# Up-projections by seven block products, and the gate through DRAM, in a two-layer encoder trunk

## The chip, the cores and the metric

The kernel runs on one core of a Trainium2 chip. The metric is the device time of one execution in microseconds (us). The kernel before ran twice, in 2821.73 and 2818.32 us; the median is 2820.03 us.

## The reference

The input x is [1024 positions, 1024 channels], float32, batch 1. There are two layers; layer 0 mixes positions by differential attention, layer 1 by windowed attention with grouped heads. After the mixer each layer has a gated MLP with a convolution over positions, then an embedding p of its own, projected and gated. In the reference's own words, with D = 1024 and D_FF = 2816:

```
def conv_ffn(h, w_up, conv_w, conv_b, w_down):
    u = h @ w_up
    up = jnp.pad(u, ((0, 0), (pad, pad), (0, 0)))
    u = sum(up[:, t:t + S] * conv_w[t] for t in range(CONV_WIDTH)) + conv_b
    gate, val = jnp.split(u, 2, axis=-1)
    return (jax.nn.silu(gate) * val) @ w_down
...
    h = h + mix
    h = h + conv_ffn(rms_norm(h, ffn_norm[i]), ...)
    gate = jax.nn.sigmoid(rms_norm(h, ple_norm[i]) @ ple_w_gate[i])
    h = h + (p[i] @ ple_w_proj[i]) * gate
return rms_norm(h, final_norm)
```

## The kernel before

Channels lie on the 128 partitions and positions along the free axis, so a row of tiles [128, 1024] holds 128 channels. Every float32 operand of a product is split into two float32r parts, hi (a cast, on ScalarE, L134) and lo (the difference, on VectorE or GpSimd, L140). `mm3` (L221) then makes three products for each pair: hi by hi, hi by lo, lo by hi (L229 to L231), each 128x128 by 128x512 into a PSUM bank.

The program goes through stages: the first norm with q, k and v of layer 0; the differential attention, 64 units of one head by 128 positions; the output projection `out_proj` (L937); the feed-forward stage `ffn` (L989); the layer's embedding with q, k, v of layer 1; the windowed attention; `out_proj` and `ffn` again; the last embedding and norm. `p_proj` (L1087) computes p @ ple_w_proj with 96 products and 16 transposes. It is a generator that is handed to both attentions as a side job: after each unit of attention one of its pieces is issued.

`out_proj` adds the projection to the residual, which comes back from DRAM (`spill`), and `norm_tile` splits h * g into hn (hi and lo, L448 and L449) and sums h * h; 1 / rms (`rstd`) is applied only later, to the products.

`ffn` has 22 column blocks j of 128. For each j, `up` loads the weight columns of the value and of the gate (1 MB), splits them, and makes for both column blocks and both halves of the positions 24 products. L1031 multiplies PSUM by rstd; the conv is one ScalarE pass (L1033) and two VectorE taps (L1037, L1041); silu is L1046, the gate's product L1047. The gated block is split into gh and gl, which stay in SBUF. After two j the products of the down-projection of the two blocks before follow (`down`), 16 sums of six products, which L1067 adds to the residual in SBUF. Up uses five PSUM banks and down three.

DMAs are issued by SyncE (SP) in program order. The order of the instructions on each engine is set when the program is built, by a scheduler that simulates time; a tile in a pool waits for the last reader of the buffer it takes.

## Time and profile before

| | |
|---|---|
| runs | 2821.73 and 2818.32 us, median 2820.03 |
| span of the profiled execution, first to last instruction | 2821.1 us |
| TensorE busy | 2742.1 us, 97% |
| VectorE, ScalarE, GpSimd busy | 1639.3, 1092.5, 901.0 us |
| feed-forward stage, first product of up to last residual add | 734.92 to 1488.58 and 1972.71 to 2724.09 us |
| granted TensorE clock, mean | 0.993 of full speed |

The page doesn't list the profiled execution's own time apart from its span; the span lies 0.6 us under the slower of the two runs. In a timeline each row is one or more instructions in sequence on one engine: start, duration, line, operation, output and inputs. In square brackets stands how long the engine had been idle and what it had waited for. A matmul's row lasts longer than the distance to the next, because products are pipelined: the distance of the starts counts. In a table of windows "(x290)" is the number of instructions.

### The profile page before, as it was taken

How to read it: one execution, taken by the hardware profiler on the slowest of the kernel's cores; microseconds unless marked ns; L12 is line 12 of the kernel's file. 1: busy time of each engine (PE TensorE's matmuls, PEld its weight loads, DVE VectorE, ACT ScalarE, POOL GpSimd, SP SyncE). 2: the span in 40 equal slices, each digit the busy share in tenths (PEclk: the TensorE clock that was granted, in tenths of full speed). 3: DMA queues.
4: the chain of work that ended last, by engine and by line, in shares of the span. 5: the costliest groups of instructions: out<-in, count | busy, mean ns of one | idle time of the engine just before them, and what ended most of it. 6: DMA issues, size and time to landing. Idle time of an engine off the chain costs nothing.

```text
span 2821.1 us, 32960 instructions
## 1 busy us (share of the span) xinstructions
PE 2742.1 (97%) x13134; PEld 2271.8 (81%) x13134; DVE 1639.3 (58%) x2010; ACT 1092.5 (39%) x1923; POOL 901.0 (32%) x555
## 2 busy tenths in 40 slices
PE   7999999999999999999999999999999999999998
PEld 6888888888888888888878788888888888888877
DVE  7540468885655555455477747774555555555574
ACT  5321576773422222222245527874322222222253
...
GB/s 222 165 164 135 156 126 108 87 23 71 60 45 46 46 59 46 45 45 45 45 45 131 140 185 186 83 72 72 60 45 48 57 45 45 45 45 46 45 72 100
DMA packets 182239, 233.30 MB, mean 83 GB/s; under 512 B 7092, under 2 KB 136261, under 8 KB 178373
## 3 DMA queue, kind: packets, MB, share of 16 engines
...
q10 hardware_dynamic: 624, 0.39, 0.0%
...
## 4 chain that ended last, share of the span: by engine, by line
PE 80%; DVE 13%; ACT 4%; issue 2%; POOL 1%; DMA 1%; SPq 0%; POOLq 0%; ACTq 0%; DVEq 0%
PE ps L229 23%; PE ps L230 23%; PE ps L231 23%; DVE c L1037 2%; PE ps L770 2%; DVE res L1067 2%; ACT e L738 1%; PE T L761 1%; PE T L902 1%; DVE sm L734 1%; PE S L732 1%; PE S L733 1%; DVE ss L674 1%; DVE c L1041 1%; DVE c L1047 1%
## 5 line engine op out<-in xcount | busy, mean ns | idle before, releaser
L140 POOL TENSOR_TENSOR wl<-wr,wh 128x1024 fp32r<-128x1024 f32 (+1 forms) x201 | 482.5, 2421 | 1479.7 <-ACT wh L134 1405.0
L229 PE MATMUL ps<-hn,wh 128*128 128x512 f32 x1952 | 761.3, 391 | 5.2 <-ACT wh L134 4.5
L230 PE MATMUL ps<-hn,wh 128*128 128x512 f32 x1952 | 760.8, 390 | 0.0
L231 PE MATMUL ps<-hn,wl 128*128 128x512 f32 x1952 | 741.4, 390 | 0.7 <-DVE wl L140 0.7
L229 PEld LDWEIGHTS ps<-hn,wh 128*128 128x128 f32 x1952 | 366.9, 188 | 84.8 <-ACT wh L134 6.7
L231 PEld LDWEIGHTS ps<-hn,wl 128*128 128x128 f32 x1952 | 366.5, 188 | 78.5 <-issue 1.4
L230 PEld LDWEIGHTS ps<-hn,wh 128*128 128x128 f32 x1952 | 366.8, 188 | 76.3 <-issue 0.5
L1031 DVE TENSOR_TENSOR us<-ps,rstd 128x512 f32<-128x512 f32 x176 | 121.6, 691 | 443.1 <-PE ps L231 441.6
L134 ACT CAST wh<-wr 128x1024 fp32r<-128x1024 f32 (+1 forms) x232 | 233.3, 1060 | 268.3 <-PE ps L230 253.5
L1067 DVE TENSOR_TENSOR res<-res,ps 128x512 f32<-128x512 f32 x352 | 234.8, 680 | 129.7 <-PE ps L231 129.7
L229 PE MATMUL ps<-gh,wh 128*128 128x512 f32 x704 | 279.0, 400 | 18.6 <-DVE res L1067 14.5
L1033 ACT ACTIVATE c<-us,conv 128x1024 f32<-128x1024 f32 x88 | 109.1, 1240 | 456.9 <-DVE us L1031 456.9
L230 PE MATMUL ps<-gl,wh 128*128 128x512 f32 x704 | 274.5, 390 | 0.0
L231 PE MATMUL ps<-gh,wl 128*128 128x512 f32 x704 | 274.5, 390 | 0.0
L1037 DVE SCALAR_TENSOR_TENSOR c<-us,conv,c 128x1023 f32<-128x1023 f32 x88 | 196.5, 2233 | 72.2 <-ACT c L1033 72.2
L734 DVE TENSOR_REDUCE sm<-S 128x1 f32<-128x1024 f32 x128 | 152.6, 1217 | 63.1 <-PE S L733 62.4
L229 PEld LDWEIGHTS ps<-gh,wh 128*128 128x128 f32 x704 | 132.0, 188 | 71.0 <-DVE res L1067 45.1
L738 ACT ACTIVATE e<-S,sm 128x1024 f32<-128x1024 f32 x128 | 142.5, 1116 | 78.1 <-DVE sm L734 75.1
L134 ACT CAST gh<-c 128x1024 fp32r<-128x1024 f32 x44 | 46.2, 1050 | 309.8 <-DVE c L1047 309.8
L231 PEld LDWEIGHTS ps<-gh,wl 128*128 128x128 f32 x704 | 132.1, 188 | 28.2
L750 POOL TENSOR_TENSOR e<-e,e 128x1024 f32<-128x1024 f32 x64 | 152.5, 2382 | 4.9
L230 PEld LDWEIGHTS ps<-gl,wh 128*128 128x128 f32 x704 | 132.2, 188 | 25.6 <-issue 0.2
...
## 6 DMA issues: line engine op xcount, KB each, us to landing
wr<-ffn_w_up SPq DMA_DIRECT2D x88, 512.0 KB, 4.4
...
qs<-rhl SPq DMA_DIRECT2D x32, 512.0 KB, 3.2
...
ks<-rhl SPq DMA_DIRECT2D x20, 512.0 KB, 3.1
spill<-res SPq DMA_DIRECT2D x16, 512.0 KB, 2.7
...
```

Of the source, the lines that this page charges most:

```text
L134: self.nc.scalar.copy(out, in_)
L140: eng.tensor_tensor(out, in_, f32(hi), op=ALU.subtract)
L229: self.nc.tensor.matmul(out, ah, bh, start=first, stop=False)
L230: self.nc.tensor.matmul(out, ah, bl, start=False, stop=False)
L231: self.nc.tensor.matmul(out, al, bh, start=False, stop=last)
L734: v.tensor_reduce(sm[:, a : a + 1], ps[:], axis=AX.X, op=ALU.max, negate=True)
L738: nc.scalar.activation(e[:], ps[:], AF.Exp, bias=sm[:, a : a + 1], accum_out=sm[:, 2 + a : 3 + a])
L750: nc.gpsimd.tensor_tensor(ea[:], ea[:], eb[:], op=ALU.add)
L1031: v.tensor_tensor(u[:, sl], ps[:], rstd[hf][:], op=ALU.mult)
L1033: nc.scalar.activation(c[:], u[:], AF.Identity, bias=self.convcol(layer, 3, f), scale=self.convcol(layer, 1, f),)
L1037: v.scalar_tensor_tensor(c[:, 1:], u[:, : S - 1], self.convcol(layer, 0, f), c[:, 1:], op0=ALU.mult, op1=ALU.add,)
L1067: v.tensor_tensor(self.res[dt][:, sl], self.res[dt][:, sl], acc[:], op=ALU.add)
```

## The change

The up-projection is seen as a product of 2x2 blocks: the weight [1024 input channels, value and gate] in two halves of the input channels by two column blocks, and the input in two halves of the channels by two halves of the positions. Seven block products of sums take the place of eight, of four matrix steps of three products each: 84 products for each j where there were 96.

`seven_inputs` makes normalised inputs first (L1004, with rstd), then the sums t1 to t4, and splits all of them. `seven_weights` makes for each j the weight sums (L1048, L1051, L1052, on GpSimd, for j < 2 on VectorE) and splits them (casts on ScalarE L1057, differences on VectorE L1058). `ffn_up` multiplies and combines the seven results from PSUM (L1143 to L1155, for j = 0 other lines); conv (L1162 to L1170), silu (L1175) and the gate's product (L1176) follow as before, and the gated block is written to DRAM (`gs`, L1177). `ffn_down` is a stage of its own: it reads the gated blocks (L1190), splits them, and in its first group takes the residual from DRAM (L1213). `p_proj` is no longer a side job; `projected` (L1378) runs it by itself between `out_proj` and the up stage. In `out_proj` hn is no longer made. Layer 1 is changed alike. Documentation strings are removed, so line numbers shift, and `dynamic_dma_scratch_size=1024` is set for the program.

```diff
--- before.py
+++ after.py
@@ -453,7 +451,8 @@
-        self.norm_split(st, kt, hf, src)
+        if st["slots"] is not None:
+            self.norm_split(st, kt, hf, src)
@@ -945,7 +944,7 @@
-        st = self.norm_begin(which, layer, hp, tp, [S_LOW, XO[0]])
+        st = self.norm_begin(which, layer, hp, tp, None)
@@ -985,51 +984,181 @@
+    def seven_inputs(self, layer, rstd, fp):
+        nc = self.nc
+        v = nc.vector
+        sub = ALU.subtract
+        out = {n: [] for n in ("b11", "b21", "b22", "t1", "t2", "t3", "t4")}
+        for kp in range(KT // 2):
+            n = []
+            for kt in (kp, kp + KT // 2):
+                t = fp.tile([P, 2, HS], F32, "t", self.nm("nh"))
+                g = self.gcol("ffn", layer, kt)
+                for hf in range(2):
+                    v.scalar_tensor_tensor(
+                        t[:, hf], self.res[kt][:, hf * HS : (hf + 1) * HS], g, rstd[hf][:],
+                        op0=ALU.mult, op1=ALU.mult,
+                    )
+                n.append(t)
+            n1, n2 = n
+            one = fp.tile([P, 2, HS], F32R, "q1", self.nm("q1"))
+            nc.scalar.copy(one[:, 0], n1[:, 0])
+            v.tensor_tensor(one[:, 1], n1[:, 0], f32(one[:, 0]), op=sub)
+            ta = fp.tile([P, 2, HS], F32, "t", self.nm("ta"))
+            tb = fp.tile([P, 2, HS], F32, "t", self.nm("tb"))
+            v.tensor_tensor(ta[:, 0], n1[:, 1], n1[:, 0], op=sub)
+            v.tensor_tensor(ta[:, 1], n2[:, 1], ta[:, 0], op=sub)
+            v.tensor_tensor(tb[:, 0], n1[:, 1], n2[:, 1], op=sub)
+            v.tensor_tensor(tb[:, 1], ta[:, 1], n2[:, 0], op=sub)
+            qa = self.resp.tile([P, 2, 2, HS], F32R, tag="res", name=self.nm("qa"))
+            qb = fp.tile([P, 2, 2, HS], F32R, "qb", self.nm("qb"))
+            qu = fp.tile([P, 2, 2, HS], F32R, "qu", self.nm("qu"))
+            for q, t in ((qa, ta), (qu, tb)):
+                nc.scalar.copy(q[:, 0], t[:])
+                v.tensor_tensor(q[:, 1], t[:], f32(q[:, 0]), op=sub)
+            nc.scalar.copy(qb[:, 0, 0], n2[:, 0])
+            nc.scalar.activation(qb[:, 0, 1], n2[:, 1], AF.Copy, scale=-1.0)
+            v.tensor_tensor(qb[:, 1, 0], n2[:, 0], f32(qb[:, 0, 0]), op=sub)
+            v.scalar_tensor_tensor(
+                qb[:, 1, 1], n2[:, 1], -1.0, f32(qb[:, 0, 1]), op0=ALU.mult, op1=sub
+            )
...
+    def seven_weights(self, raw, fp, hurry):
+        nc = self.nc
+        v = raw[:].rearrange("p (b c) -> p b c", b=4)
+        sf = fp.tile([P, 4, HS], F32, "sf", self.nm("sf"))
+        eng = nc.vector if hurry else nc.gpsimd
+        eng.tensor_tensor(
+            sf[:, 0:2], v[:, 2].unsqueeze(1).to_broadcast([P, 2, HS]), v[:, 0::3], op=ALU.add
+        )
+        eng.tensor_tensor(sf[:, 2], sf[:, 1], v[:, 0], op=ALU.add)
+        eng.tensor_tensor(sf[:, 3], sf[:, 2], v[:, 1], op=ALU.add)
+        out = {}
+        def split(src, names, tile_):
+            t = tile_[:].rearrange("p (e b c) -> p e b c", e=2, c=HS)
+            self.nc.scalar.copy(t[:, 0], src)
+            nc.vector.tensor_tensor(t[:, 1], src, f32(t[:, 0]), op=ALU.subtract)
+            for i, n in enumerate(names):
+                out[n] = (t[:, 0, i], t[:, 1, i])
+        big = lambda: self.ring.tile(
+            [P, WSZ], F32R, tag="wh" if self.flip() else "wl", name=self.nm("w7")
+        )
+        split(v[:, 0:2], ("a11", "a12"), big())
+        split(sf[:, 2:4], ("s2", "s4"), big())
+        split(sf[:, 0:2], ("s3", "s1"), big())
+        split(v[:, 3:4], ("a22",), fp.tile([P, 2 * HS], F32R, "wd", self.nm("wd")))
+        return out
+    def product(self, ps, w, x, kps, first, last):
...
+    def ffn_up(self, layer, x7, fp, psum, gs):
         nc = self.nc
...
+        kps = range(KT // 2)
+        for j in range(FT):
+            raw = self.ring.tile([P, WSZ], F32, tag="wr", name=self.nm("wr"))
+            r = raw[:].rearrange("p (t k c) -> p t k c", t=2, k=KT)
             for t in range(2):
+                nc.sync.dma_start(
+                    r[:, t],
+                    wu[:, (t * FT + j) * P : (t * FT + j + 1) * P].rearrange(
+                        "(k p) c -> p k c", p=P
+                    ),
+                )
+            w = self.seven_weights(raw, fp, j < 2)
+            bank = lambda: psum.tile([P, HS], F32, "ps", self.nm("ps"))
+            small = lambda: fp.tile([P, HS], F32, "e", self.nm("e"))
+            ug = fp.tile([P, S], F32, "t", self.nm("ug"))
+            uv = fp.tile([P, S], F32, "t", self.nm("uv"))
+            lo, hi = slice(0, HS), slice(HS, S)
+            pairs = {
+                "m1": ("a11", "b11"), "m2": ("a12", "b21"), "m3": ("s4", "b22"),
+                "m4": ("a22", "t4"), "m5": ("s1", "t1"), "m6": ("s2", "t2"), "m7": ("s3", "t3"),
+            }
+            def prod(ps, m, first=True):
+                a, b = pairs[m]
+                self.product(ps[:], w[a], x7[b], kps, first, True)
+            if j == 0:
...
+            else:
+                pa, pb, pc, pd, pe = (bank() for _ in range(5))
+                t1, t2, t3 = small(), small(), small()
+                prod(pa, "m1")
+                nc.scalar.copy(t1[:], pa[:])
+                prod(pb, "m6")
+                v.tensor_tensor(t2[:], pb[:], t1[:], op=ALU.subtract)
+                prod(pd, "m7")
+                v.tensor_tensor(t3[:], t2[:], pd[:], op=ALU.add)
+                prod(pc, "m5")
+                v.tensor_tensor(uv[:, hi], t3[:], pc[:], op=ALU.add)
+                prod(pa, "m2", False)
+                nc.scalar.copy(ug[:, lo], pa[:])
+                prod(pe, "m4")
+                v.tensor_tensor(uv[:, lo], t3[:], pe[:], op=ALU.subtract)
+                prod(pc, "m3", False)
+                v.scalar_tensor_tensor(
+                    ug[:, hi], t2[:], -1.0, pc[:], op0=ALU.mult, op1=ALU.subtract
+                )
+            cs = [None, None]
+            for t, u in ((1, uv), (0, ug)):
                 f = t * FT + j
...
+                c = fp.tile([P, S], F32, "t", self.nm("c"))
                 nc.scalar.activation(
@@ -1042,13 +1171,27 @@
-                cs.append(c)
+                cs[t] = c
...
+            nc.sync.dma_start(gs[j][:], cs[0][:])
+    def ffn_down(self, layer, gs, hp, tp, psum, which, nlayer, rc=None):
+        nc = self.nc
+        v = nc.vector
+        wd = self.io["ffn_w_down"][layer]
+        groups = FT // 2
+        st = self.norm_begin(which, nlayer, hp, tp, [S_LOW, XO[0]])
+        self.res = [None] * KT
+        gts = {}
+        def load(j):
+            raw = tp.tile([P, S], F32, tag="t", name=self.nm("gr"))
+            nc.sync.dma_start(raw[:], gs[j][:])
...
-            self.copy_hi(hi[:], cs[0][:])
-            self.sub_lo(v, lo[:], cs[0][:], hi[:])
+            self.copy_hi(hi[:], raw[:])
+            self.sub_lo(v, lo[:], raw[:], hi[:])
@@ -1056,7 +1199,7 @@
-                acc = psum.at(DOWN_BANKS[(hf * KT + dt) % 3], [P, HS], F32, self.nm("ps"))
+                acc = self.bank(psum)
@@ -1064,28 +1207,41 @@
-                v.tensor_tensor(self.res[dt][:, sl], self.res[dt][:, sl], acc[:], op=ALU.add)
+                if g == 0:
+                    self.rows_tile(self.res, dt, "res")
+                    old = tp.tile([P, HS], F32, tag="n", name=self.nm("old"))
+                    nc.sync.dma_start(old[:], self.spill[dt * P : (dt + 1) * P, sl])
+                    v.tensor_tensor(self.res[dt][:, sl], old[:], acc[:], op=ALU.add)
+                else:
+                    v.tensor_tensor(self.res[dt][:, sl], self.res[dt][:, sl], acc[:], op=ALU.add)
...
+        dblk = {}
+        def fetch(g):
+            self.hurry = g == 0
+            dblk[g] = self.wrows(wd, 2 * g * P, 2, 0, D)
+            self.hurry = False
+            for j in (2 * g, 2 * g + 1):
+                load(j)
+        fetch(0)
...
-            up(2 * g)
-            up(2 * g + 1)
-            if g > 0:
-                for hf in range(2):
-                    down(g - 1, hf, False)
-            dblk[g] = self.wrows(wd, 2 * g * P, 2, 0, D)
-        for hf in range(2):
-            down(groups - 1, hf, True)
-            self.norm_half(st, hf, psum, ["b4"])
-            if rc is not None:
-                self.rstd_cols(st["rstd"][hf], hf, rc, psum, ["b4"])
+            if g + 1 < groups:
+                fetch(g + 1)
+            for hf in range(2):
+                down(g, hf, g == groups - 1)
+                if g == groups - 1:
+                    self.norm_half(st, hf, psum, END_BANKS)
+                    if rc is not None:
+                        self.rstd_cols(st["rstd"][hf], hf, rc, psum, END_BANKS)
@@ -1214,10 +1370,34 @@
...
+    def projected(self, layer, w, out_pp, next_norm):
+        io = self.io
+        gs = [self.dram.tile([P, S], F32, name=self.nm("gs")) for _ in range(FT)]
+        with ExitStack() as c:
+            tp, hp = self.stage(c, f"w{layer}", XO[0] + XO[1])
+            psum = self.banks(c, f"w{layer}")
+            rstd = self.out_proj(w, hp, tp, psum, "ffn", layer)
+            self.spill_res()
+            for _ in self.p_proj(
+                layer, out_pp, psum, BANKS,
+                lambda n: tp.tile([P, S], F32, tag="t", name=n),
+            ):
+                pass
+        with ExitStack() as c:
+            fp = self.slots(
+                c, f"u{layer}",
+                {"q1": 4, "qb": 4, "qu": 4, "sf": 1, "wd": 2, "t": 5, "e": 4},
+            )
+            psum = self.slots(c, f"pu{layer}", {"ps": 8}, PSUM)
+            x7 = self.seven_inputs(layer, rstd, fp)
+            self.ffn_up(layer, x7, fp, psum, gs)
+        return gs
@@ -1271,19 +1451,13 @@
-            side = self.p_proj(
-                0, pp[0], psum, END_BANKS,
-                lambda n: ap.pools["e"].tile([P, S], F32, tag="e", bufs=EBUF, name=n),
-            )
-            self.diff_attn(ap, psum, [side])
+            self.diff_attn(ap, psum, [])
+        gs = self.projected(0, io["diff_w_o"][0], pp[0], "ple")
...
-                hn, rstd = self.ffn(0, hn, rstd, hp, tp, psum, "ple", 0)
+                hn, rstd = self.ffn_down(0, gs, hp, tp, psum, "ple", 0)
```

Three places show how instructions move. The first is VectorE where the up stage begins in layer 0; `wl`, `w_1121`, `w_1123`, `wd` are lo parts of weights, `nh` a normalised input, `sf` a weight sum, `nacc` the sum of squares. Before:

```order
L140 TENSOR_TENSOR wl_6462<-wr_6458,wh_6461 128x512 x2
L449 SCALAR_TENSOR_TENSOR hn_6345<-res_6167,par,hn_6345 128x512
L464 TENSOR_TENSOR nacc_5944<-nacc_5944,old_6342 128x512
L965 TENSOR_TENSOR res_6234<-ps_6383,old_6408 128x512
L464 TENSOR_TENSOR nacc_5944<-nacc_5944,old_6375 128x512
L140 TENSOR_TENSOR wl_6595<-wr_6591,wh_6594 128x512 x2
L449 SCALAR_TENSOR_TENSOR hn_6411<-res_6234,par,hn_6411 128x512
L464 TENSOR_TENSOR nacc_5944<-nacc_5944,old_6408 128x512
```

In the change, from the end of the norm's second half on:

```order
L468 SCALAR_TENSOR_TENSOR nv_6182<-nv_6182 128x512
L469 SCALAR_TENSOR_TENSOR rstd_6186<-nv_6182,rstd_6186 128x512
L1058 TENSOR_TENSOR w_1121_6527<-wr_6520,w_1121_6527 128x1024
L1004 SCALAR_TENSOR_TENSOR nh_6416<-res_5687,par,rstd_6056 128x512
L1004 SCALAR_TENSOR_TENSOR nh_6416<-res_5687,par,rstd_6186 128x512
L1004 SCALAR_TENSOR_TENSOR nh_6419<-res_5957,par,rstd_6056 128x512
L1004 SCALAR_TENSOR_TENSOR nh_6419<-res_5957,par,rstd_6186 128x512
L1048 TENSOR_TENSOR sf_6523<-wr_6520 128x1024
L1058 TENSOR_TENSOR wd_6536<-wr_6520,wd_6536 128x512
L1058 TENSOR_TENSOR wd_6671<-wr_6655,wd_6671 128x512
L1015 TENSOR_TENSOR ta_6425<-nh_6416 128x512
```

Ahead of the up stage VectorE now has no hn split left, and all work on the inputs follows after the second half's rstd, with weight work of j = 0 and 1 among it.

The second place is VectorE in the middle of the stage, one j. Before, with adds of the down-projection (`res`) between (`us` is the product times rstd, `c` the conv):

```order
L1031 TENSOR_TENSOR us_8374<-ps_8401,rstd_6420 128x512
L1067 TENSOR_TENSOR res_6018<-res_6018,ps_8590 128x512
L1067 TENSOR_TENSOR res_6167<-res_6167,ps_8606 128x512
L1037 SCALAR_TENSOR_TENSOR c_8427<-us_8374,conv,c_8427 128x1023
L1067 TENSOR_TENSOR res_6234<-res_6234,ps_8622 128x512
L1041 SCALAR_TENSOR_TENSOR c_8427<-us_8374,conv,c_8427 128x1023
L1047 TENSOR_TENSOR c_8370<-c_8370,c_8427 128x1024
L1067 TENSOR_TENSOR res_6234<-res_6234,ps_8614 128x512
L140 TENSOR_TENSOR gl_8434<-c_8370,gh_8433 128x1024
L1031 TENSOR_TENSOR us_8446<-ps_8447,rstd_6278 128x512
```

In the change (`e`, `ug` and `uv` are combinations of PSUM banks; `w_` and `wd` are lo parts of the weights of later j):

```order
L1147 TENSOR_TENSOR e_7076<-e_7075,ps_7072 128x512
L1153 TENSOR_TENSOR uv_7068<-e_7076,ps_7073 128x512
L1149 TENSOR_TENSOR uv_7068<-e_7076,ps_7071 128x512
L1058 TENSOR_TENSOR w_1232_7317<-wr_7310,w_1232_7317 128x1024
L1166 SCALAR_TENSOR_TENSOR c_7168<-uv_7068,conv,c_7168 128x1023
L1170 SCALAR_TENSOR_TENSOR c_7168<-uv_7068,conv,c_7168 128x1023
L1145 TENSOR_TENSOR e_7206<-ps_7201,e_7205 128x512
L1155 SCALAR_TENSOR_TENSOR ug_7067<-e_7075,ps_7071 128x512
L1058 TENSOR_TENSOR w_1216_7192<-sf_7182,w_1216_7192 128x1024
L1166 SCALAR_TENSOR_TENSOR c_7172<-ug_7067,conv,c_7172 128x1023
L1170 SCALAR_TENSOR_TENSOR c_7172<-ug_7067,conv,c_7172 128x1023
L1176 TENSOR_TENSOR c_7172<-c_7172,c_7168 128x1024
```

The adds of the down-projection and the split of the gate have left, and a j now has four weight differences and five combinations.

The third place is the queue of DMAs on SP between up and down of layer 0. Before, in the same stage, weight loads alternate:

```order
L161 DMA wr_7126<-ffn_w_up 128x8x128 x2
L161 DMA wr_7255<-ffn_w_up 128x8x128 x2
L161 DMA wr_7512<-ffn_w_down 128x2x1024
L161 DMA wr_7520<-ffn_w_up 128x8x128 x2
L161 DMA wr_7649<-ffn_w_up 128x8x128 x2
L161 DMA wr_7906<-ffn_w_down 128x2x1024
```

In the change, from the last but one gated block on (`gs` the gated blocks in DRAM, `gr` their read, `old` the residual from `spill`):

```order
L1177 DMA gs_5523<-c_9268 128x1024
L159 DMA wr_9863<-ffn_w_down 128x2x1024
L1177 DMA gs_5524<-c_9399 128x1024
L1190 DMA gr_9519<-gs_5503 128x1024
L1190 DMA gr_9525<-gs_5504 128x1024
L1190 DMA gr_9539<-gs_5505 128x1024
L1190 DMA gr_9545<-gs_5506 128x1024
L1213 DMA old_9559<-spill_6192 128x512
L1213 DMA old_9569<-spill_6192 128x512
L1190 DMA gr_9723<-gs_5507 128x1024
...
L1213 DMA old_9580<-spill_6192 128x512
```

The first reads of gated blocks stand behind the write of the last one, and most loads of the residual behind the reads of four more.

## Rows read from the trace of the kernel before

**Rows 1.** Page, part 1: busy time, share of span, instructions of each engine.
```profile
PE 2742.1 (97%) x13134; PEld 2271.8 (81%) x13134; DVE 1639.3 (58%) x2010; ACT 1092.5 (39%) x1923; POOL 901.0 (32%) x555
```

**Rows 2.** Windows, feed-forward stage: us, then each engine's busy time, PEclk, DMA, GB/s.
```profile
1008.68:1075.75 67.07, 66.18 (x290) 53.82 (x289) 34.73 (x36) 15.01 (x15) 14.29 (x7) 1.00 0.16 47
```

**Rows 3.** Timeline of PE in up: start us, us, operation; 18 products left out.
```profile
1001.64 0.39 PE L231 MATMUL ps<-hn,wl 128*128 128x512 f32 x1
...
1005.95 0.39 PE L231 MATMUL ps<-hn,wl 128*128 128x512 f32 x1
```

**Rows 4.** Timeline of POOL, the same stage: a weight block's subtraction.
```profile
1008.68 4.76 POOL L140 TENSOR_TENSOR wl<-wr,wh 128x1024 fp32r<-128x1024 f32 x2 [22.48 <-ACT wh L134]
```

**Rows 5.** Timeline of DVE, the same stage.
```profile
1009.09 0.69 DVE L1067 TENSOR_TENSOR res<-res,ps 128x512 f32<-128x512 f32 x1 [0.67 <-PE ps L231]
1011.06 3.46 DVE L1037 SCALAR_TENSOR_TENSOR c<-us,conv,c 128x1023 f32<-128x1023 f32 x1
...
1015.04 1.27 DVE L1041 SCALAR_TENSOR_TENSOR c<-us,conv,c 128x1023 f32<-128x1023 f32 x1
```

**Rows 6.** Timeline of PE: first product of up, layer 0 and layer 1.
```profile
734.92 0.39 PE L229 MATMUL ps<-hn,wh 128*128 128x512 f32 x1
...
1972.71 0.39 PE L229 MATMUL ps<-hn,wh 128*128 128x512 f32 x1
```

**Rows 7.** Timeline of DVE: last residual add of down, layer 0 and 1.
```profile
1488.58 0.68 DVE L1067 TENSOR_TENSOR res<-res,ps 128x512 f32<-128x512 f32 x1
...
2724.09 0.68 DVE L1067 TENSOR_TENSOR res<-res,ps 128x512 f32<-128x512 f32 x1
```

**Rows 8.** Timeline of POOL in layer 0's attention, one L750 for each unit.
```profile
375.91 2.37 POOL L750 TENSOR_TENSOR e<-e,e 128x1024 f32<-128x1024 f32 x1
...
400.29 2.37 POOL L750 TENSOR_TENSOR e<-e,e 128x1024 f32<-128x1024 f32 x1
...
435.80 2.36 POOL L750 TENSOR_TENSOR e<-e,e 128x1024 f32<-128x1024 f32 x1
...
456.06 2.36 POOL L750 TENSOR_TENSOR e<-e,e 128x1024 f32<-128x1024 f32 x1
```

**Rows 9.** Windows: layer 1's attention.
```profile
1760.00:1860.00 100.00, 98.64 (x606) 87.41 (x605) 82.24 (x146) 89.04 (x246) 44.94 (x80) 1.00 0.19 67
```

**Rows 10.** Groups of one shape: count, busy, mean ns; then idle before, releaser.
```profile
L1033 ACT ACTIVATE c<-us,conv 128x1024 f32<-128x1024 f32 x88 | 109.1, 1240 | 456.9 <-DVE us L1031 456.9
...
L140 DVE TENSOR_TENSOR gl<-c,gh 128x1024 fp32r<-128x1024 f32 x44 | 53.6, 1218 | 14.8 <-ACT gh L134 14.8
...
L134 ACT CAST gh<-c 128x1024 fp32r<-128x1024 f32 x44 | 46.2, 1050 | 309.8 <-DVE c L1047 309.8
```

**Rows 11.** DMA view, issues: count, KB each, us from issue to landing.
```profile
pp<-pp SPq DMA_DIRECT2D x16, 512.0 KB, 2.6
old<-spill SPq DMA_DIRECT2D x32, 256.0 KB, 2.7
```

**Rows 12.** Timeline of DVE: back to back ops, and a wait for ScalarE.
```profile
741.52 0.74 DVE L449 SCALAR_TENSOR_TENSOR hn<-res,par,hn 128x512 fp32r<-128x512 f32 x1
742.18 0.68 DVE L464 TENSOR_TENSOR nacc<-nacc,old 128x512 f32<-128x512 f32 x1
...
749.00 0.68 DVE L1031 TENSOR_TENSOR us<-ps,rstd 128x512 f32<-128x512 f32 x1
749.60 0.68 DVE L469 SCALAR_TENSOR_TENSOR nv<-nv 128x512 f32<-128x512 f32 x1
...
1335.20 1.28 DVE L1037 SCALAR_TENSOR_TENSOR c<-us,conv,c 128x1023 f32<-128x1023 f32 x1 [1.37 <-ACT c L1033]
```

**Rows 13.** Windows after a pause of PE in layer 1's attention.
```profile
1875.00:1880.00 5.00, 5.00 (x22) 4.14 (x21) 2.94 (x7) 2.93 (x6) 1.87 (x3) 0.69 0.00 0
```

**Rows 14.** Timeline of PE in that window.
```profile
1876.79 0.78 PE L229 MATMUL ps<-wh,wh 128*128 128x512 f32 x1
1877.36 0.63 PE L230 MATMUL ps<-wl,wh 128*128 128x512 f32 x1
```

More of the change, by code (lines that the diff above doesn't have):

```diff
@@ L102 @@
 MIX_BANKS = ["b4", "b2", "b5", "b3"]
-UP_BANKS = ["b0", "b1", "b6", "b7", "b4"]
-DOWN_BANKS = ["b5", "b2", "b3"]
 class Trunk:
@@ L986, in half_order @@
             done(hf)
-    def ffn(self, layer, hn, rstd, hp, tp, psum, which, nlayer, rc=None):
+    def seven_inputs(self, layer, rstd, fp):
[36 more added lines that the diff above has]
+            )
+            out["b11"].append((one[:, 0], one[:, 1]))
+            for name, q, i in (
+                ("b21", qb, 0), ("b22", qb, 1), ("t1", qa, 0),
+                ("t2", qa, 1), ("t3", qu, 0), ("t4", qu, 1),
+            ):
+                out[name].append((q[:, 0, i], q[:, 1, i]))
+        return out
@@ new lines, in flip @@
+    def flip(self):
+        self.turn = not getattr(self, "turn", False)
+        return self.turn
+    def product(self, ps, w, x, kps, first, last):
+        terms = [
+            (w[0][:, k * P : (k + 1) * P], w[1][:, k * P : (k + 1) * P], x[k][0], x[k][1])
+            for k in kps
+        ]
+        n = len(terms)
+        for i, (ah, al, bh, bl) in enumerate(terms):
+            mm = self.nc.tensor.matmul
+            mm(ps, ah, bh, start=first and i == 0, stop=False, skip_group_check=True)
+            mm(ps, ah, bl, start=False, stop=False, skip_group_check=True)
+            mm(ps, al, bh, start=False, stop=last and i == n - 1, skip_group_check=True)
@@ L1281, in run @@
             with ExitStack() as c:
-                psum = self.banks(c, "w0")
-                hn, rstd = self.out_proj(io["diff_w_o"][0], hp, tp, psum, "ffn", 0)
-            with ExitStack() as c:
                 psum = self.banks(c, "f0")
-                hn, rstd = self.ffn(0, hn, rstd, hp, tp, psum, "ple", 0)
+                hn, rstd = self.ffn_down(0, gs, hp, tp, psum, "ple", 0)
             with ExitStack() as c:
@@ L1294, in run @@
             psum = Bank(c, self.tc, "ps_a1", ["S0", "b2", "b3", "b4", "b5", "S1"], PSUM)
-            side = self.p_proj(
-                1, pp[1], psum, MIX_BANKS,
-                lambda n: ap.pools["a"].tile([P, S], F32, tag="a", bufs=6, name=n),
-            )
-            self.swa(ap, psum, [side])
+            self.swa(ap, psum, [])
+        gs = self.projected(1, io["swa_w_o"][0], pp[1], "ple")
         with ExitStack() as sc:
@@ L1302, in run @@
             with ExitStack() as c:
[L1303 to L1305 removed]
                 psum = self.banks(c, "f1")
                 rcol = self.cp.tile([P, 8], F32, name="rcol2")
[L1308 removed]
+                hn, rstd = self.ffn_down(1, gs, hp, tp, psum, "ple", 1, rcol)
             with ExitStack() as c:
```

69 lines of the change are left out of this document (25 added, 44 removed).

## The prediction, made before the changed kernel ran

> **What bounds the kernel now.** First the page's busy row [rows 1]: TensorE is busy 97% of the 2821.1 us span, so a change is worth what it takes off TensorE less the pauses it makes. Then the table of windows in the feed-forward stage [rows 2]: one group (two column blocks j of the up-projection and one group of the down-projection, 288 products) lasts 67.07 us. A product of 512 columns starts every (1005.95 - 1001.64) / 19 = 0.2268 us [rows 3]; 288 of them are 65.3 us, so only 1.8 us in 67 (2.7%) is lost. Where it is lost the timelines of VectorE and GpSimd show: from 1008.68 GpSimd subtracts for 4.76 us [rows 4], and the conv tap L1037 that starts at 1011.06 takes 3.46 us where the next takes 1.27 [rows 5]; the adds L1067 that free the down-projection's banks queue behind it. The add at 1009.09, which reads PSUM, takes 0.69 us though GpSimd is busy. So an instruction of VectorE with both operands in SBUF waits for GpSimd's, and one on PSUM does not.
>
> The stage runs from its first product to its last residual add: 734.92 to 1488.58 and 1972.71 to 2724.09 [rows 6, 7], that is 753.7 and 751.4 us, 1505.0 together. There is no pause ahead of it: the first up-product follows out_proj's last at once.
>
> **What is removed.** Per block j 84 products stand for 96: 12 x 22 x 2 = 528 fewer, 528 x 0.2268 = 119.7 us. The multiplications by 1/rms (L1031) go, and so do the stalls at three down banks, as the down stage has eight. The side job p_proj leaves both attentions. Layer 0: with it four units (the L750 at 375.91 to that at 400.29) take 24.4 us, later without it 20.3 (435.80 to 456.06) [rows 8], 1.03 us for each of 16 to 20 units: 18 us, between 16 and 20.6. Layer 1 has it nearly throughout; there TensorE is busy 98.6 of 100 us and ScalarE 89 [rows 9]. Its 96 products and the transposes are 22.8 us, the upper end; if ScalarE's chain sets the pace it gives nothing, the lower. I take 12. Together -30.
>
> **What is added, per layer.**
> *p_proj by itself*: 96 x 0.2268 = 21.8, some 1 for 16 transposes and 2 for its first casts (estimates): 24.8.
>
> *First pause, p_proj to up.* VectorE's first normalising op (L1004) writes to a tile of the next pool, in the memory that p_proj's output tiles held, so it waits for the last output transfer: about 1.05 us for the ScalarE cast ahead [rows 10], 0.6 for the PSUM copy (half of the 1.24 of a 1024-wide pass [rows 10]), 2.6 for the transfer [rows 11] and hops, 4.6 us after p_proj's last product. Everything of seven_inputs and of the first weights is queued behind it on VectorE: 20 ops like L449 at 0.66 (741.52 to 742.18), 30 of 512 columns at 0.60 (749.00 to 749.60) [rows 12], 13 subtractions of 1024 at 1.22 [rows 10]: 13.2 + 18.0 + 15.9 = 47.1, and 2 for ScalarE's casts between. Of the 168 products of j = 0 and 1 about 108 (24.5 us) can run meanwhile, as their operands come. TensorE stands 4.6 + 47.1 + 2 - 24.5, and 2 for the last operand's chain: 31. Low clock comes on top: after its pause before 1876 us TensorE had a granted clock of 0.69 (partly the 1.2 GHz level), and products started 0.57 us apart (1876.79, 1877.36) for some us [rows 13, 14]; that costs about 2.5 us. **34** in all, between 28 and 44.
>
> *Up.* j = 0 and 1: 168 x 0.2268 = 38.1. The other 20 cost 84 x 0.2268 = 19.05 each if TensorE sets the pace. VectorE's list for one j is three subtractions and the gate product at 1.22, one of 512 at 0.69, four conv taps at 1.28, five combinations from PSUM at 0.69: 4.9 + 0.7 + 5.1 + 3.5 = 14.2. GpSimd's three weight sums are 2 x 2.38 = 4.76 by [rows 4], and where they meet SBUF work one side waits: 18.96 at most, just under 19.05. I take the loss that the stage has now, 2.7%: 19.56 x 20 = **391.2**. The bounds are 19.05 and the rival below.
>
> Here a page speaks against the change. The Trainium skill (GPSIMD Engine Reference, 4.1 Engine selection) says to do an elementwise sum on VectorE, as GpSimd takes about twice as long for two inputs, and (8. Key points) that the two share SBUF interfaces when a VectorE op has two SBUF inputs. The trace agrees on both: 2.38 against 1.22 us, and 3.46 against 1.27. By that rule, with the sums on VectorE, the list would be 14.2 + 2.4 = 16.6 us, clear of 19.05.
>
> *Second pause, up to down.* After the last product of j = 21 come the last combination (0.69), conv on ScalarE (1.24) behind casts (1.05 each), two taps (1.28 each) that take turns with GpSimd's 2 x 2.38, silu (taken as a cast, 1.05), gate product (1.22): about 10.5 us by [rows 4, 5, 10]. On SP the reads of the first gate blocks are queued behind the write of this last one, so they are issued only now: 2.7 us to land [rows 11], a cast and hops: TensorE restarts after about 15. The residual's loads stand behind four block reads and have two buffers: (2.7 + 0.7) / 2 = 1.7 us each against 6 x 0.2268 = 1.36 of a down sum, 0.34 x 14 = 4.8 lost, less if the eight banks absorb it. With 2.5 of clock: **22**, between 14 and 32.
>
> *Down.* 1056 x 0.2268 = 239.5. Its end is VectorE's: norm work beside the adds as now, about 9.
>
> The DRAM trip of the gate costs nothing inside a stage: one 512 KB write takes 2.6 us [rows 11] and has a period of 19.6 us to itself, and a read is issued a group ahead; uncovered it would cost that 2.6, as it does in the second pause. VectorE and ScalarE lose the split of hn in out_proj, where TensorE is never idle: nothing.
>
> **Sum.** 24.8 + 34 + 38.1 + 391.2 + 22 + 239.5 + 9 = 758.6 per layer, 1517.2 for two against 1505.0: +12.2, less 30 in attention: -17.8. The profiled span becomes 2803.3. The span lies 1.1 us above the median of 2820.03 (runs of 2818.32 and 2821.73), so the median becomes **2802 us**: the 120 us that the products save are spent at two new pauses and on p_proj by itself.
>
> **Rivals.**
> 1. *The saving goes through* (13%). The up period is 19.05 (-10.2 a layer), the pauses 28 and 14 (-14), and attention gives 43.4 (-13.4): 2802 - 48.4 - 13.4 = 2740. For it: TensorE loses only 2.7% now. Against it: every term at its good end at once.
> 2. *VectorE becomes the bound in up* (20%), slower than before. Its list and GpSimd's sum to 18.96, and twice for each j VectorE waits for ScalarE's conv: at 1335.20 it had stood 1.37 us for that [rows 12]. If nothing fills these waits the period is 18.96 + 2.74 = 21.7, and 40 x (21.7 - 19.56) = 86 more: 2888. It decides from 21.4 a block, where the time passes 2% above now. By the two rules of the Trainium skill above (GPSIMD Engine Reference) the sums on GpSimd are the wrong side to put them. The trace bears out the sharing, not that the waits stay empty. Against it: the order puts other subtractions of the next block between.
> 3. *Longer pauses* (15%): 44 and 32, that is +20 a layer: 2842. For it: both sit behind transfers and one VectorE queue with no other work to run. It stays within 2%.
> My own case has 52%.
>
> **Numbers.** A measurement of this kernel tells about 2% (56 us) from no change, so faster is below 2764 and slower above 2876. Faster 0.13 (rival 1), slower 0.20 (rival 2), within 0.67 (forecast and rival 3). The range 2750 to 2890 takes in rival 3, rival 2 at its price and most of rival 1. The forecast's own range is 2775 to 2840.
>
> **What would show it.** Attention units of 5.07 us from the first one in layer 0; TensorE idle for about 31 us after p_proj's last product, with the first L1004 released by a transfer; 84 products every 19.1 to 20 us in up, without a wait for L1058 or for a bank longer than 0.5 us; TensorE idle for some 15 to 20 us before the down stage, released by the gate block's read; then 21.8 us for each down group. The prediction is wrong if the up period is above 21 us (VectorE releases TensorE at every block), or if either pause is outside its bounds.

## The result

The changed kernel takes 2790.16 us (2789.81 and 2790.52), the kernel before 2820.03. The ratio is 0.989, interval 0.9862 to 0.9919: 30 us less, within the 2% that count as no change here. The forecast was 2802, in a range from 2750 to 2890.

The page of the changed kernel, span and part 1, answers to [rows 1]:

```profile
span 2788.7 us, 33239 instructions
...
PE 2644.0 (95%) x12606; PEld 2183.4 (78%) x12606; DVE 1958.8 (70%) x2314; ACT 1210.2 (43%) x2101; POOL 1016.0 (36%) x587
```

TensorE's busy time fell by 98 us, the span by 32.4. VectorE is busy 320 us longer, its waits for GpSimd counted. Where the rest went is read at the stage's borders, as in [rows 6, 7]. The timeline of TensorE in layer 0 has the first work of p_proj, its last product, the first of up, the last of up and the first of down:

```profile
722.59 0.60 PE L1256 MATMUL ps<-identr,wr 128*128 128x128 f32 x4
...
748.83 0.39 PE L229 MATMUL ps<-wh,wl 128*128 128x512 f32 x1
754.89 0.80 PE L1084 MATMUL ps<-q,w 128*128 128x512 f32 x1 [5.67 <-ACT q L1011]
...
1201.25 0.39 PE L1086 MATMUL ps<-qb,w 128*128 128x512 f32 x1
1217.86 0.79 PE L227 MATMUL ps<-gh,wh 128*128 128x512 f32 x1 [16.22 <-ACT gh L132]
```

The same five in layer 1:

```profile
1935.46 0.71 PE L1256 MATMUL ps<-identr,wr 128*128 128x128 f32 x5
...
1962.34 0.39 PE L229 MATMUL ps<-wh,wl 128*128 128x512 f32 x1
1968.35 0.80 PE L1084 MATMUL ps<-q,w 128*128 128x512 f32 x1 [5.62 <-ACT q L1011]
...
2414.66 0.39 PE L1086 MATMUL ps<-qb,w 128*128 128x512 f32 x1
2431.15 0.80 PE L227 MATMUL ps<-gh,wh 128*128 128x512 f32 x1 [16.10 <-ACT gh L132]
```

The last residual adds on VectorE in both layers:

```profile
1476.08 0.69 DVE L1216 TENSOR_TENSOR res<-res,ps 128x512 f32<-128x512 f32 x1 [0.51 <-PE ps L229]
...
2692.14 0.69 DVE L1216 TENSOR_TENSOR res<-res,ps 128x512 f32<-128x512 f32 x1 [3.02 <-PE ps L229]
```

A last product occupies 0.23 us more than its start. With that the terms of the prediction come out as follows (us):

| term | predicted | layer 0 | layer 1 |
|---|---|---|---|
| p_proj by itself | 24.8 | 26.5 | 27.1 |
| pause ahead of up and thin first blocks | 34 | 33.3 | 33.2 |
| 22 blocks of up | 429.3 | 419.1 | 419.1 |
| second pause, down and its end | 270.5 | 274.6 | 277.3 |
| sum | 758.6 | 753.5 | 756.7 |
| sum before | | 753.7 | 751.4 |

The second row is the time from p_proj's end to up's end, less 22 x 19.05, so whatever up loses stands in it; where that lies follows below. The two stages together are 5.1 us longer than before (12.2 forecast). All the gain lies ahead of the two stages, where the attentions are: out_proj's last product is reached 12.3 us sooner in layer 0 and a further 24.8 in layer 1, together 37.1 (30 forecast). 37.1 - 5.1 and 0.4 behind the last add make the 32.4.

**Up** runs at TensorE's pace. One block in the window view, to be held against [rows 2]:

```profile
930.01:949.05 19.04, 19.04 (x86) 15.77 (x85) 16.67 (x15) 7.96 (x10) 7.82 (x3) 1.00 0.28 83
```

84 products of up are 19.04 us, and TensorE is busy in all of it, as in the whole 318.84 us from 861.16 to 1180.00. VectorE is busy 16.67 us, with its waits for GpSimd in it. In the timeline of VectorE a free conv tap, then one beside GpSimd, and the gate product (answers to [rows 5]):

```profile
936.85 1.28 DVE L1170 SCALAR_TENSOR_TENSOR c<-uv,conv,c 128x1023 f32<-128x1023 f32 x1
...
942.12 3.30 DVE L1170 SCALAR_TENSOR_TENSOR c<-ug,conv,c 128x1023 f32<-128x1023 f32 x1
946.62 1.22 DVE L1176 TENSOR_TENSOR c<-c,c 128x1024 f32<-128x1024 f32 x1 [1.19 <-ACT c L1175]
```

GpSimd's three weight sums in the same stretch:

```profile
941.01 3.33 POOL L1048 TENSOR_TENSOR sf<-wr 128x1024 f32<-128x1024 f32 x1 [11.07 <-DVE w L1058]
944.42 2.16 POOL L1051 TENSOR_TENSOR sf<-sf,wr 128x512 f32<-128x512 f32 x1
946.66 2.33 POOL L1052 TENSOR_TENSOR sf<-sf,wr 128x512 f32<-128x512 f32 x1
```

The tap at 942.12 takes 3.30 us, the one at 936.85 takes 1.28; the first sum takes 3.33. Both engines wait in turn, and at this length of the lists TensorE does not notice: it is busy in all of the 19.04 us.

**The pause ahead of up**, windows of layer 0 (columns as in [rows 2]):

```profile
722.00:740.00 18.00, 16.81 (x79) 13.03 (x78) 7.36 (x10) 12.54 (x20) 5.18 (x2) 1.00 0.63 196
740.00:760.00 20.00, 11.04 (x44) 8.13 (x43) 7.79 (x11) 9.37 (x15) 0.00 (x0) 0.86 0.41 165
760.00:780.00 20.00, 15.59 (x39) 9.65 (x39) 20.00 (x28) 8.27 (x11) 0.00 (x0) 0.63 0.19 52
780.00:800.00 20.00, 16.56 (x56) 10.97 (x56) 20.00 (x29) 8.72 (x11) 0.00 (x0) 0.91 0.19 52
```

TensorE is busy 11.04, 15.59 and 16.56 of 20 us, partly at 1.2 GHz (clock 0.86, 0.63, 0.91), while VectorE, from 753 on, works without a gap. On ScalarE the first weight cast, and on VectorE the first and the last operations of its queue:

```profile
749.07 1.04 ACT L1057 CAST w<-wr 128x1024 fp32r<-128x1024 f32 x1 [0.55 <-PE ps L228]
750.15 1.22 DVE L1058 TENSOR_TENSOR w<-wr,w 128x1024 fp32r<-128x1024 f32 x1 [15.13 <-ACT w L1057]
753.43 2.74 DVE L1004 SCALAR_TENSOR_TENSOR nh<-res,par,rstd 128x512 f32<-128x512 f32 x4 [2.06 <-DMA pp<-pp]
...
799.93 1.23 DVE L1024 TENSOR_TENSOR qu<-tb,qu 128x1024 fp32r<-128x1024 f32 x1
```

VectorE had stood 15.13 us, for a weight cast that waits for a ring tile until p_proj's last products have read it, and 2.06 more for the transfer of p_proj's last output. rstd had been ready at 735.0. The queue on the inputs ends at 801.16; by then TensorE has made 101 products of up in 52.1 us, so 29.2 of the 33.3 us are lost here. Another 2.1 go in a later block that waits for its weights (1.32 us at 838.04), and 1.8 in the last block, which waits for VectorE (1.65 us at 1198.58).

**The second pause** on SP, VectorE and ScalarE:

```profile
1208.45 0.37 SPq L159 DMA_DIRECT2D wr<-ffn_w_down  x1
1211.94 0.34 SPq L1177 DMA_DIRECT2D gs<-c  x1
1212.37 2.91 SPq L1190 DMA_DIRECT2D gr<-gs  x4
```

```profile
1206.26 3.24 DVE L1170 SCALAR_TENSOR_TENSOR c<-ug,conv,c 128x1023 f32<-128x1023 f32 x1
1210.69 1.23 DVE L1176 TENSOR_TENSOR c<-c,c 128x1024 f32<-128x1024 f32 x1 [1.18 <-ACT c L1175]
```

```profile
1216.76 1.04 ACT L132 CAST gh<-gr 128x1024 fp32r<-128x1024 f32 x1 [6.10 <-DMA gr<-gs]
```

The last gate product runs at 1210.69, its write is issued at 1211.94, the four reads behind it from 1212.37, and the first cast follows at 1216.76, after its transfer. TensorE stands 16.22 us.

### The profile page after: what moved, and what is told of

It is laid out like the page before. It is cut to its first block, busy times and chain, and to the rows that moved or that the text cites. A ratio compares the mean times of both kernels' runs of the same rounds, so it can differ in the third digit from the quotient of the medians.

```text
span 2788.7 us, 33239 instructions
## 1 busy us (share of the span) xinstructions
PE 2644.0 (95%) x12606; PEld 2183.4 (78%) x12606; DVE 1958.8 (70%) x2314; ACT 1210.2 (43%) x2101; POOL 1016.0 (36%) x587
## 5 line engine op out<-in xcount | busy, mean ns | idle before, releaser
L138 POOL TENSOR_TENSOR wl<-wr,wh 128x1024 fp32r<-128x1024 f32 (+1 forms) x113 | 293.1, 2609 | 817.6 <-ACT wh L132 743.9
L1048 POOL TENSOR_TENSOR sf<-wr 128x1024 f32<-128x1024 f32 x40 | 128.4, 3210 | 585.3 <-DVE w L1058 585.3
L1216 DVE TENSOR_TENSOR res<-res,ps 128x512 f32<-128x512 f32 x320 | 216.6, 684 | 140.4 <-PE ps L229 140.4
L227 PE MATMUL ps<-hn,wh 128*128 128x512 f32 x544 | 214.7, 396 | 5.6 <-ACT wh L132 4.9
L228 PE MATMUL ps<-hn,wh 128*128 128x512 f32 x544 | 212.9, 392 | 0.0
L229 PE MATMUL ps<-hn,wl 128*128 128x512 f32 x544 | 212.4, 392 | 0.1
L132 ACT CAST wh<-wr 128x1024 fp32r<-128x1024 f32 (+1 forms) x140 | 144.9, 1091 | 121.5 <-PE ps L228 62.7
L132 ACT CAST gh<-gr 128x1024 fp32r<-128x1024 f32 x44 | 46.2, 1050 | 343.3 <-PE ps L229 328.9
L1057 ACT CAST w<-sf 128x1024 fp32r<-128x1024 f32 x88 | 92.6, 1052 | 174.4 <-PE ps L1086 106.6
L229 PEld LDWEIGHTS ps<-gh,wl 128*128 128x128 f32 x704 | 133.0, 189 | 27.9
L749 POOL TENSOR_TENSOR e<-e,e 128x1024 f32<-128x1024 f32 x64 | 152.3, 2380 | 5.2
L1084 PE MATMUL ps<-qa,w 128*128 128x512 f32 x352 | 138.6, 397 | 10.5 <-ACT qa L1023 8.1
L1084 PE MATMUL ps<-qb,w 128*128 128x512 f32 x352 | 140.2, 398 | 6.0 <-DVE uv L1149 3.3
L1086 PE MATMUL ps<-qa,w 128*128 128x512 f32 x352 | 138.9, 395 | 2.6 <-DVE w L1058 2.6
L1085 PE MATMUL ps<-qa,w 128*128 128x512 f32 x352 | 139.3, 396 | 0.0
```

The lines of the kernel that those rows point to most:

```text
L132: self.nc.scalar.copy(out, in_)
L138: eng.tensor_tensor(out, in_, f32(hi), op=ALU.subtract)
L227: self.nc.tensor.matmul(out, ah, bh, start=first, stop=False)
L228: self.nc.tensor.matmul(out, ah, bl, start=False, stop=False)
L229: self.nc.tensor.matmul(out, al, bh, start=False, stop=last)
L749: nc.gpsimd.tensor_tensor(ea[:], ea[:], eb[:], op=ALU.add)
```

## The experiments

Each ran beside the kernel before, and the ratio to it is what is compared; the changed kernel has 0.989. The diffs are shortened: `...` stands for lines and arguments left out.

**1. p_proj back into the attentions.**

```diff
-            for _ in self.p_proj(...): pass
...
-            self.diff_attn(ap, psum, [])
+            self.diff_attn(ap, psum, [side])
...
-            self.swa(ap, psum, [])
+            self.swa(ap, psum, [side])
```

> p_proj goes back into both attentions as a side job; all else as changed. Theory (the terms of the prediction with their measured sizes): the two stages of p_proj by itself (26.5 us each, 722.59 to 749.06) go, -53; the attentions give back what they gained, +12.3 and +24.8; and the norm chain of about 12 us after out_proj's last product (rstd ready at 735.0) is no longer covered by TensorE work, which makes the pause ahead of up about 8 us longer in each layer, +16. Sum 0: 2790, between 2782 and 2798. Rival: what p_proj costs by itself is pure loss and its work was nearly free in attention: 2750 to 2765.

Measured: 2793.15 us, ratio 0.9894 (0.9879 to 0.9909). The attentions reach out_proj's end 16.9 and 27.9 us later, and the stages are 19.3 and 20.7 shorter. They are not 26.5 shorter, as TensorE now stands while the norm is made:

```profile
739.22 0.39 PE L229 MATMUL ps<-xo,wl 128*128 128x512 f32 x1
741.83 1.67 PE L488 MATMUL ps<-nacc,ones 128*128 128x512 f32 x2 [2.22 <-DVE nacc L463]
750.50 0.80 PE L1084 MATMUL ps<-q,w 128*128 128x512 f32 x1 [7.00 <-ACT q L1011]
```

From 739.22 to 750.50 there are only two products of the norm. So p_proj in the attentions costs 44.8 us and by itself, with what it covers, 40.0; taking it out moved the time and saved nothing that can be told apart. The theory holds; the prediction's size of layer 1's share does not (12 was forecast).

**2. The wait for p_proj's transfer taken away.** Another tile order in the pool:

```diff
+        qus = [fp.tile([P, 2, 2, HS], F32R, "qu", self.nm("qu")) for _ in range(KT // 2)]
...
-            qu = fp.tile([P, 2, 2, HS], F32R, "qu", self.nm("qu"))
+            qu = qus[kp]
```

> The tiles t3, t4 of the inputs take the memory in which p_proj's output tiles lay, so the normalised inputs no longer wait for p_proj's last output transfer; order of work unchanged. Theory: the wait alone is worth what VectorE stood for it, 2.06 us in each layer: 2786, since VectorE's queue behind it and the weight split ahead of it stay. Rival: the transfer sets the whole 6 us in which TensorE stands before its first up product, and the queue behind it moves by as much: 2778 or less.

Measured: 2787.04, ratio 0.9872 (0.9855 to 0.9888), whose interval overlaps the changed kernel's. VectorE's timeline:

```profile
749.98 1.23 DVE L1059 TENSOR_TENSOR w<-wr,w 128x1024 fp32r<-128x1024 f32 x1 [15.15 <-ACT w L1058]
751.12 1.41 DVE L1005 SCALAR_TENSOR_TENSOR nh<-res,par,rstd 128x512 f32<-128x512 f32 x2
```

No wait stands ahead of the normalisation any more, and the first up product comes 30.4 us after out_proj's last and not 32.5: the 2.1 us of the theory, at the start of up. They do not last. Up's last product comes 478.3 and 477.4 us after out_proj's last where it came 478.9 and 479.4, as the third and fourth gate product of layer 0 come 1.6 us later than this start would have them, and the whole stages are only 0.0 and 0.8 us shorter in the profiled execution. So it is shown that the wait delayed the start of up, not that it cost 2.1 us a layer; the times alone don't tell it either.

**3. p_proj beside the work on the inputs.**

```diff
-            for _ in self.p_proj(...): pass
...
             x7 = self.seven_inputs(layer, rstd, fp)
+            for _ in self.p_proj(layer, out_pp, psum, BANKS, fp):
+                pass
```

p_proj's results also leave in halves of 512 columns.

> p_proj is issued after the work on the inputs, in the same pool (its results leave in halves of 512 columns), so VectorE normalises and sums from the moment rstd is there, about 735 us, and not from 753, while TensorE does p_proj. Theory: VectorE's queue of 47 us is what fills the pause, so 18 us of it move under p_proj, of which some is lost as p_proj's own four VectorE subtractions come later: -15 to -18 in each layer, 2754 to 2760. Rival: the weights of the first block (ring tiles that p_proj holds to its end) or ScalarE's casts set the start of up: 2782 or more.

Measured: 2766.46, ratio 0.9799 (0.9784 to 0.9813): 24 us less than the changed kernel, and between the theory and the rival. The windows of the same stretch:

```profile
722.00:740.00 18.00, 12.57 (x46) 9.02 (x45) 12.73 (x14) 10.67 (x15) 5.46 (x2) 0.81 0.42 124
740.00:760.00 20.00, 17.86 (x77) 14.19 (x76) 20.00 (x31) 16.00 (x26) 0.00 (x0) 0.98 0.63 227
760.00:780.00 20.00, 19.47 (x75) 14.38 (x75) 20.00 (x26) 8.07 (x12) 0.00 (x0) 0.94 0.35 98
780.00:800.00 20.00, 18.85 (x80) 14.47 (x80) 18.51 (x22) 9.89 (x11) 6.18 (x3) 1.00 0.14 39
```

VectorE is full from 740 to 780, and TensorE is busy 17.86, 19.47 and 18.85 of 20. p_proj's first product, its last, and up's first:

```profile
730.92 0.50 PE L230 MATMUL ps<-wh,wh 128*128 128x512 f32 x1 [1.89 <-ACT wh L135]
...
755.84 0.39 PE L232 MATMUL ps<-wh,wl 128*128 128x512 f32 x1
757.19 0.50 PE L1087 MATMUL ps<-q,w 128*128 128x512 f32 x1 [0.96 <-ACT w L1060]
```

From out_proj's last product to the last add it is 742.5 and 745.0 us, against 753.7 and 756.9 in the changed kernel: 11 to 12 us a layer, under the 15 to 18 expected. p_proj itself ends later, at 756.1 and not at 749.1, mostly because it starts later: its first product comes 9.0 us after out_proj's last and not 2.5, since the norm's two products now stand ahead of its transposes and the norm's two activations ahead of its weight casts on ScalarE. VectorE's queue on the inputs starts at 734.69 and ends at 786.21, where it ran from 753.43 to 801.16, and the pause shrinks with it. That this queue sets the pause is shown by its place in time; no run made the queue itself shorter.

**4. The reads of gated blocks issued early**, on top of experiment 2.

```diff
-            nc.sync.dma_start(gs[j][:], cs[0][:])
+            (nc.scalar if j >= FT - 2 else nc.sync).dma_start(gs[j][:], cs[0][:])
...
-            self.nc.sync.dma_start(view, src)
+            (self.nc.scalar if self.late else self.nc.sync).dma_start(view, src)
```

(`late` is set for the third and fourth down weights.)

> As the run without the wait, and in addition the last two gate writes and the loads of the third and fourth down weights are issued by ScalarE, so that SP issues the first reads of gated blocks and of the residual without standing behind them. Theory: TensorE's second pause of 16.4 us shrinks by what the reads come earlier, to the last gate product plus one cast: about 12 us, and the next three blocks are there already: -5 to -7 in each layer against the run without the wait, 2772 to 2776. Rival: the pause is the chain conv, silu, gate product, cast on VectorE and ScalarE, and the transfer is a small part of it: within 2 us a layer, 2782 or more.

Measured: 2780.48, ratio 0.9851 (0.9837 to 0.9866): 6.6 us under experiment 2, which ran on the same chip. That is about half of the theory's 5 to 7 in each layer, and above its 2772 to 2776. SP issues the reads 8.6 us ahead of up's last product and not 11.1 behind it, and the pause is 11.8 us:

```profile
1189.58 3.33 SPq L1192 DMA_DIRECT2D gr<-gs  x4
```

```profile
1198.16 0.39 PE L1088 MATMUL ps<-qb,w 128*128 128x512 f32 x1
1210.32 1.22 PE L228 MATMUL ps<-gh,wh 128*128 128x512 f32 x2 [11.77 <-ACT gh L133]
```

```profile
1209.22 3.88 ACT L133 CAST gh<-gr 128x1024 fp32r<-128x1024 f32 x4 [1.66 <-DVE c L1178]
```

What is left is the chain of the last block on VectorE and ScalarE, since ScalarE casts the first gated block behind it, and behind the last write that ScalarE now issues (1208.85). It stood idle for 4.79 us ahead of the last silu and 1.66 ahead of the casts, so part of the rest is the order on ScalarE; no run changed that. Of 16.2 us the queue on SP was 4.5. From up's last product to the last add the stretch is 4.6 and 5.0 us shorter than in experiment 2, in one execution each.

**5. Experiments 3 and 4 together.** The edits are those of 3 and of 4 with 2.

> The last two changes together: p_proj beside the work on the inputs, and the early reads of gated blocks. Theory: the pauses are apart from each other, so their gains add: 2766.5 less the 6.5 that the early reads gave = 2760, between 2756 and 2764. Rival: one pause's work moves into the other's place (longer transfers, later weights): 2766 or more.

Measured: 2753.48 us (2752.67 to 2755.83), ratio 0.9765 (0.975 to 0.978), the fastest of all: 2.35% under the kernel before, which is clear of 2%, and 1.3% under the changed one. The gains add: the ratios of experiments 3 and 4, each against the changed kernel's, would make 0.976. The time is below the expected 2756 to 2764, which counted experiment 4 over experiment 2 although the edit of experiment 2 is in this run too.

**6. Weight sums on VectorE.**

```diff
-            w = self.seven_weights(raw, fp, j < 2)
+            w = self.seven_weights(raw, fp, True)
```

> As changed, but the weight sums of all blocks are made on VectorE, none on GpSimd in up. The Trainium skill (GPSIMD Engine Reference, 4.1 Engine selection) has them there. Theory: up is set by TensorE at 19.04 us a block with either, as VectorE is busy 16.66 of 19.04 us including its waits for GpSimd: 2790, within 3. Rival: sharing with GpSimd costs somewhere (the first or last blocks, a late weight): 2780 or less; or VectorE's added 2.4 us stand in the way of a bank: 2800 or more.

Measured: 2790.38, ratio 0.9896 (0.9878 to 0.9913). One block:

```profile
930.00:949.04 19.04, 19.04 (x85) 15.77 (x84) 15.95 (x18) 7.87 (x10) 0.00 (x0) 1.00 0.27 82
```

The same 19.04 us. VectorE is busy 15.95 us where it was 16.67, though it does three sums more: without GpSimd's work it has none to wait for. The sums are 1.14 + 0.60 + 0.60, by the distances of starts (0.60 for 512 columns [rows 12], 1.14 for 1024). Less these, VectorE's own list is 13.6 us, not 14.2.

**7. GpSimd's first sum made twice.**

```diff
+        if not hurry:
+            eng.tensor_tensor(
+                sf[:, 0:2], v[:, 2].unsqueeze(1).to_broadcast([P, 2, HS]), v[:, 0::3], op=ALU.add
+            )
```

> As changed, but GpSimd makes its first sum of 1024 columns twice for 20 of 22 blocks, 2.4 us more a block by a free GpSimd. Theory A (the prediction's sum, every VectorE op excludes GpSimd): 14.2 + 4.76 + 2.38 = 21.3 us a block, 40 x 2.3 = 92 more: 2880. Theory B (only ops with both operands in SBUF exclude it, the five combinations from PSUM and VectorE's idle time do not count): 14.2 - 3.5 + 7.1 = 17.9, still under TensorE's 19.04: 2790 to 2800.

Measured: 2840.08, ratio 1.007 (1.0055 to 1.0085). Neither theory: 50 us more.

```profile
930.92:951.16 20.24, 19.35 (x86) 15.71 (x85) 17.30 (x16) 7.97 (x9) 10.15 (x5) 1.00 0.27 79
```

A block takes 20.24 us: 2.38 more work for GpSimd cost 1.2. VectorE is busy 17.30 of it, TensorE 19.35, so TensorE no longer sets the pace. If what is added beyond the edge counts in full, up was some 1.2 us a block from its edge (an estimate).

**8. The same with two sum tiles.**

```diff
-                {"q1": 4, "qb": 4, "qu": 4, "sf": 1, "wd": 2, "t": 5, "e": 4},
+                {"q1": 4, "qb": 4, "qu": 4, "sf": 2, "wd": 2, "t": 5, "e": 4},
```

> As the run with the first sum made twice, but the weight sums have two tiles in turn and not one, so GpSimd needn't wait for VectorE's last difference of the block before. That run's period was 20.23 us a block: GpSimd's four sums, 10.4 us, and then 9.85 until VectorE had read the last of them. Theory: that ring through the one tile sets the period, and with two tiles it is TensorE's again: 19.05, and 2840 less 40 x 1.19 = 2792. Rival: VectorE's list with its waits for GpSimd and ScalarE sets it: 20 or more, 2830 to 2840.

Measured: 2850.2, ratio 1.0094 (1.0077 to 1.0111). The theory of a ring through the one tile falls:

```profile
929.89:950.03 20.14, 19.33 (x86) 15.68 (x85) 19.61 (x16) 7.97 (x9) 9.97 (x4) 1.00 0.25 79
```

20.14 us with VectorE busy in 19.61. Its own 13.6 leave 6.0 us, which are waits for GpSimd, beside 7.1 us of GpSimd's work. This fits the list and the sharing as the limit, the rival here and rival 2 of the prediction; no run took the sharing away at this load. The 10 us more than in experiment 7, at a period that is a little shorter, arise in the first blocks: layer 0's first gate product comes 81.0 us after p_proj's last product, there 74.8, and the shorter period wins back only part. Why the first blocks are slower stays open.

**9. One product of the seven made a second time.** TensorE's count in these blocks is again that of the plain form (the sum then holds this product twice).

```diff
                 prod(pe, "m4")
+                prod(pe, "m4", False)
```

> As changed, but one of the seven products is made and added a second time in 21 of 22 blocks of each layer (its result is then not the reference's), so TensorE has 96 products a block as before, and all else is the new form: staging, sums, pauses. Theory: each product is worth its full 0.2267 us: 504 x 0.2267 = 114 more, 2904, and the new form without the saving costs 84 us more than the kernel before. Rival: up has stalls that the products fill: 2890 or less.

Measured: 2900.86, ratio 1.0287 (1.0272 to 1.0303): 111 us more than the changed kernel for 504 products, 0.22 us each.

```profile
930.00:951.76 21.76, 21.76 (x98) 18.03 (x97) 15.71 (x15) 8.41 (x9) 7.81 (x3) 1.00 0.24 73
```

A block is 96 products, 21.76 us. So the products saved are worth nearly their full time, 97% of 0.2268 us each, and the new form by itself (stages apart, sums, two pauses, p_proj alone) costs 81 us over the kernel before.

## Why the prediction was right, point by point

- *The saving of 120 us is spent on pauses and on p_proj.* Right, and shown from both sides: experiment 9 gives 111 us for the products, experiments 3 and 4 give back parts of the pauses. p_proj by itself is 53.6 us, but against its place in the attentions it makes no difference in time (experiment 1), so on balance it is the pauses that take most of the saving.
- *First pause 34.* Measured 33.3 and 33.2. The mechanism is as predicted: VectorE's queue starts 4.4 us after p_proj's last product (4.6 forecast) and lasts 47.7 (49.1 with the casts), and 101 products run beside it (108): 29.2 us, for 31. Of the late start the transfer is only 2.1 us; the rest is the weight split ahead of it in VectorE's order, which stands for p_proj's ring tile. The prediction counted the time right and named only the transfer. The low clock did not come on top, as forecast with 2.5: from 755 to 774 us the granted clock was 0.50 (1.2 GHz), TensorE having stood since 749.2, and VectorE's queue ran throughout. Instead two later blocks of up lose 3.9. So the total is met partly by luck. In layer 0 TensorE's waits sum to 18 us, and not to the 31 named as a sign, since the products between them run slowly.
- *Second pause 22.* 16.4 and 16.3, and in the first two down groups 5.3 and 3.8 (48.8 and 47.3 us against 43.5): 21.7 and 20.1. The chain of 10.5 us is there: from 1201.48 to 1211.9.
- *Up at 19.56.* This term was mis-sized: 19.04. The 2.7% were carried over from the stage of before, but they were the wait for three down banks behind L1067, which the prediction itself had just taken out. In the window of [rows 2] three starts of down products (1042.37, 1044.17, 1045.90) hold 1.7 of the 1.8 us lost, and no product of up holds any. That is -10 us a layer. The longest of the three:

```profile
1042.37 0.50 PE L229 MATMUL ps<-gh,wh 128*128 128x512 f32 x1 [0.68 <-DVE res L1067]
```

- *Rival 2, VectorE as the bound at 21.7.* Not so here. Its sum of 18.96 took each op at its length and the waits for ScalarE on top; the list is 13.6 us, and the free margin is about 1.2 us a block (experiment 7). The sharing itself is as the prediction had it. The rule of the Trainium skill (GPSIMD Engine Reference, 4.1 Engine selection) that elementwise sums go on VectorE changes nothing here: experiment 6 follows it at equal time. By the Trainium skill (GPSIMD Engine Reference, 8. Key points) the two engines contend when a VectorE op has two SBUF inputs; the trace agrees, 1.28 against 3.30 us.
- *Attention -30.* 37.1. Layer 1's 12 was a middle between two bounds; 24.8 came, above the upper one of 22.8. 3.5 of it lie in out_proj itself (87.9 us from first to last product, before 91.4), which experiment 1 has too, with p_proj back. That p_proj was on the path in layer 1 is shown by experiment 1 (27.9 us when it returns); through which engine is not shown. Layer 0's pace came as read (the first 20 units 20.9 us faster; 16 to 20.6 forecast), but the first unit's L749 starts 4.6 us later than its L750 before, and from the last unit to out_proj's last product it takes 94.7 us where it took 85.7. Experiment 1 has 94.7 as well, so it is not p_proj. Before, out_proj's first product stood 10.5 us ahead of the last unit's L750 (638.78 and 649.27), now it stands 4.7 behind its L749 (632.64 and 627.94): out_proj no longer begins between the last units. What moved it in the scheduler's order is open.
- *p_proj 24.8, down's end 9.* 26.5 and 27.1, and the last down group takes 13.5 and 17.8 us over the others.
- *Rivals 1 and 3.* Of rival 1 the period of 19.05 came, but not its pauses of 28 and 14, nor its 43.4 in attention. The pauses of rival 3 did not come.

The errors have both signs; what brought the time below the forecast is the up term (-20 us) and layer 1's attention (-13), less layer 0's attention (+6) and some 13 in p_proj, the pauses and down. That is 14.6 us in the span (2788.7 for 2803.3); in the median it is 12, as the span now lies 1.5 us under the median and was taken 1.1 above it.
